# Source order on three more engines in the token mixers of a hybrid decoder layer, with projection weights loaded ahead, six streams and sums a tick later

## Chip, cores and metric

One core of one Trainium2 chip (trn2). The time is the device time of one execution in microseconds; lower is better. The kernel takes its inputs as they are and does all arithmetic on the chip in one launch.

## What is computed

One inference step of a decoder layer, width 1024, for a prompt of 1024 tokens and a sample group of 8 sequences with 4 new tokens each (32 columns), which share the weights. From the reference, cut:

```
h = x + 0.5 * _swiglu(_rmsnorm(x, g_ffn1), w_ffn1_in, w_ffn1_out)
u = _rmsnorm(h, g_mix)
z_swa, z_gq, z_gk, z_gv, z_gr, z_ga, z_mq = jnp.split(u @ w_in, SPLIT_POINTS, axis=-1)
# branch A, 3 groups (window, dilation) = (128,1), (512,4), (2048,16) x 4 heads of 128
q, k = _rope(qkv[:, :, 0], pos), _rope(qkv[:, :, 1], pos)
...  # per group: softmax over a band of 129 keys at stride dil, its output and log-denominator
o_swa = jnp.sum(softmax(stack(lses), axis=0)[..., None] * stack(outs), axis=0)
# branch B, gated linear attention: 4 heads, d_k 64, d_v 128, chunks of 64
# branch C, 4 heads of attention into 256 memory tokens
gates = jax.nn.sigmoid(u @ w_gate).reshape(B, T, N_BRANCH, D_MODEL)
h = h + jnp.sum(gates * einsum(stack([o_swa, o_gla, o_mem]), w_branch), axis=2) @ w_out
h = h + 0.5 * _swiglu(_rmsnorm(h, g_ffn2), w_ffn2_in, w_ffn2_out)
```

Prompt queries see the prompt's own keys. The sample's queries see cached keys and values of 8 sequences (up to 2048 positions in the third group, 256 memory positions in branch C), each sequence its own. All matrices are float32.

## The kernel before

The 1056 columns (1024 of the prompt, 32 of the sample) lie features on partitions, in NC = 3 chunks of C = 352. A float32 product is made of three matmuls on rounded halves: weights and activations are split into a high part and the rest, and `product` (L194 to L204) issues wh·xh (L202), wh·xl (L203) and wl·xh (L204) for each 128 rows of the contraction: 24 matmuls of 352 columns for a chunk of a projection out of `w_in`. `weights` (L177) makes the two halves: a load into `raw` (L174, issued by SyncE, SP), a cast on ScalarE into `whi` (L188), a subtraction on VectorE into `wlo` (L189). Each of the three tiles has two buffers (`WBUFS`). Big intermediate rows live in 34 slabs of 128 x 1056 floats, given out in turn, with a tag each use. PSUM has four `acc` and four `aux` buffers.

The mixers are the class `Mix`, its course in `run` (L1620): the four GLA heads with the memory projections, then for each head h and each group g a dilated-attention unit. `swa_unit` (L1301) makes the unit's three projections through `proj` (L778): weights first, then per chunk `tick`, `product`, and the evacuation. Queries and keys leave through `rope` (L1281): three VectorE products out of PSUM (L1289 to L1291), one sum on GpSimd (L1295), and a GpSimd sum for the sample's columns (L1297).

All else runs in **streams**: generators in five queues, of which `tick` (L100) advances each by one step before every chunk of a projection. So a unit of nine ticks carries, between its 24-matmul products, the steps of

- `swa_unit_attention` (L1321), the unit before: scores on TensorE (L1343) with a masked maximum on VectorE (L1348), softmax (VectorE nm L1353, ScalarE exponential L1356), transposes and their copies (pt, L1086 on ScalarE, L1088 on VectorE), values (L1384);
- `mem_head` (L1108), attention into the memory: scores, exponential (L1141), reciprocal and scaling (mml L1143, mp L1145), transposes, values (its inputs are split again: mqs, mpt L208, L209); behind it in the same queue `mem_sample` (L1185): products of cached memory keys and queries on GpSimd (mqb, L1204), their sums on VectorE (msc, L1205), transposes (L1211), a softmax (msp);
- `swa_sample_scores` (L1458): per cached sequence a load of the query rows and one of the cached keys into the slab kq (L1465, L1467, L1470), a product on GpSimd (kq, L1481), its sum on VectorE (ssc, L1482); `swa_sample` (L1488) then turns ssc on TensorE (L1494) and weighs the cached values (L1546);
- `swa_combine` (L1559): the three groups' weights (sd, cd and cb are trips through DRAM), products on VectorE and GpSimd (og, L1614) and sums on both (og, L1616).

TensorE takes the order in which the program is written (`manual_schedule` with PE alone, L1892). VectorE, ScalarE, GpSimd and SP take the order in which the framework's scheduler puts their instructions, by its own estimate of when each can run. `gated_branches` (L1650) follows; the last streams run on within it.

## Time and profile before

| | us |
|---|---|
| median of 3 runs | 3043.07 (3041.36 to 3049.46) |
| profiled execution | 3053.2 |
| its span on the core | 3051.4 |
| granted TensorE clock, mean over the span | 0.975 |
| busy: VectorE, ScalarE, GpSimd | 1415.2, 1013.6, 972.3 |

The span is read from the start of the execution's first instruction. A little after 790 us the GLA part begins, dilated attention runs from about 1100 to 1757, the gated branches from there to 1860; the feed-forward halves lie ahead and behind. Since one engine is busy nearly all the time, its waits and its clock are to be read, and of the others only what ends such a wait.

### The profile page before, as it was taken

The numbers are of one execution on the slowest core, as the hardware profiler recorded it, in microseconds if no ns is written. First come the engines' busy times: TensorE is split into PE (matmuls) and PEld (weight loads), VectorE is DVE, ScalarE is ACT, GpSimd is POOL, SyncE is SP. The second block draws the span as 40 slices with busy tenths as digits, with TensorE's granted clock in tenths as the row PEclk, the third lists the DMA queues.
The fourth block names the chain that finished last, engine by engine and source line by source line (L and its number), as shares of the span: only waits on it lengthen the run. The fifth ranks groups of instructions, "written<-read, shape, count | busy, mean of one in ns | idle before, by whom it ended". The sixth has DMA issues, their size and how long they took to land. (4 is left out here: it accounts for less than half of the span.)

```text
span 3051.4 us, 51965 instructions
## 1 busy us (share of the span) xinstructions
PE 2932.9 (96%) x21035; PEld 2867.0 (94%) x21035; DVE 1415.2 (46%) x2581; ACT 1013.6 (33%) x2007; POOL 972.3 (32%) x835
## 2 busy tenths in 40 slices
PE   8999999999999999899998889999999999999999
PEld 7999999899999999888897789999999999999998
DVE  7544444454424445656556551213246544444544
ACT  5433333221345433232332321212234433333212
POOL 4533331110401114637447350112236433332000
PEclk9999999999999999999999889999999999999999
DMA  5222224432211124666566563211252222225322
GB/s 180 80 73 82 78 79 154 151 119 67 92 43 57 58 71 131 174 164 195 150 182 189 166 189 105 81 42 56 75 168 85 78 78 82 73 78 194 96 62 86
DMA packets 455604, 332.88 MB, mean 109 GB/s; under 512 B 34850, under 2 KB 417284, under 8 KB 455364
## 3 DMA queue, kind: packets, MB, share of 16 engines
q1 hardware_dynamic: 445698, 323.44, 34.9%
q10 hardware_dynamic: 9666, 6.11, 0.7%
q8 instruction: 165, 2.70, 0.4%
q14 instruction: 75, 0.61, 0.1%
HBM read 268.88 MB, written 60.60 MB: 108 GB/s over the span
## 5 line engine op out<-in xcount | busy, mean ns | idle before, releaser
L202 PE MATMUL acc<-xh,whi 128*128 128x352 f32 x1776 | 600.0, 338 | 1.4 <-ACT whi L188 1.0
L204 PE MATMUL acc<-xh,wlo 128*128 128x352 f32 x1776 | 587.6, 331 | 8.1 <-DVE wlo L189 8.1
L203 PE MATMUL acc<-xl,whi 128*128 128x352 f32 x1776 | 586.0, 330 | 0.0
L202 PEld LDWEIGHTS acc<-xh,whi 128*128 128x128 f32 x1776 | 345.8, 195 | 13.5 <-issue 9.5
L204 PEld LDWEIGHTS acc<-xh,wlo 128*128 128x128 f32 x1776 | 344.4, 194 | 13.9 <-DVE wlo L189 13.9
L203 PEld LDWEIGHTS acc<-xl,whi 128*128 128x128 f32 x1776 | 345.4, 194 | 0.2
L188 ACT CAST whi<-raw 128x512 fp32r<-128x512 f32 (+2 forms) x200 | 163.3, 816 | 541.1 <-PE acc L203 467.6
L202 PE MATMUL acc<-hh,whi 128*128 128x352 f32 (+2 forms) x968 | 313.8, 324 | 3.0 <-ACT mv L628 1.6
L203 PE MATMUL acc<-hl,whi 128*128 128x352 f32 (+2 forms) x968 | 312.9, 323 | 2.9 <-POOL hl L209 2.1
L204 PE MATMUL acc<-hh,wlo 128*128 128x352 f32 (+2 forms) x968 | 312.9, 323 | 0.9 <-DVE wlo L189 0.9
L189 DVE TENSOR_TENSOR wlo<-raw,whi 128x512 fp32r<-128x512 f32 (+2 forms) x200 | 221.2, 1106 | 176.0 <-ACT whi L188 157.4
L202 PE MATMUL acc<-xs,swf 128*128 128x264 f32 x960 | 276.1, 288 | 8.6 <-ACT u L430 8.6
L203 PE MATMUL acc<-xs,swf 128*128 128x264 f32 x960 | 274.7, 286 | 0.0
L204 PE MATMUL acc<-xs,swf 128*128 128x264 f32 x960 | 274.6, 286 | 0.0
L662 DVE SCALAR_TENSOR_TENSOR h<-acc,h 128x352 f32<-128x352 f32 (+3 forms) x296 | 150.2, 512 | 220.8 <-PE acc L204 219.7
L202 PE MATMUL acc<-xs,whi 128*128 128x264 f32 x768 | 220.9, 288 | 2.5 <-ACT xs L208 1.9
L203 PE MATMUL acc<-xs,whi 128*128 128x264 f32 x768 | 220.8, 288 | 0.8 <-POOL xs L209 0.8
L202 PEld LDWEIGHTS acc<-xs,swf 128*128 128x128 f32 x960 | 182.3, 190 | 9.9 <-ACT u L430 9.9
L202 PEld LDWEIGHTS acc<-hh,whi 128*128 128x128 f32 x968 | 182.8, 189 | 4.3 <-ACT mv L628 1.9
L203 PEld LDWEIGHTS acc<-hl,whi 128*128 128x128 f32 x968 | 182.9, 189 | 3.6 <-POOL hl L209 2.3
L204 PEld LDWEIGHTS acc<-hh,wlo 128*128 128x128 f32 x968 | 182.8, 189 | 1.2 <-DVE wlo L189 1.2
L203 PEld LDWEIGHTS acc<-xs,swf 128*128 128x128 f32 x960 | 182.8, 190 | 0.0
(427 smaller groups left out, 6743.5 us busy)
## 6 DMA issues: line engine op xcount, KB each, us to landing
raw<-in_w_ffn_in SPq DMA_DIRECT2D x88, 512.0 KB, 3.9
raw<-in_w_in SPq DMA_DIRECT2D x52, 512.0 KB, 3.9
kq<-sqt SPq DMA_DIRECT2D x96, 256.0 KB, 5.5
hraw<-hidd SPq DMA_DIRECT2D x44, 528.0 KB, 3.9
raw<-in_w_ffn_out SPq DMA_DIRECT2D x64, 256.0 KB, 2.8
kq<-in_cache_swa SPq DMA_DIRECT2D x64, 256.0 KB, 5.1
vc<-in_cache_swa SPq DMA_DIRECT2D x64, 256.0 KB, 4.6
raw<-in_w_gate SPq DMA_DIRECT2D x24, 512.0 KB, 4.2
```

What stands on the lines that cost most here:

```text
L188: nc.scalar.copy(hi[:, :n], raw[:, :n])
L189: nc.vector.tensor_sub(lo[:, :n], raw[:, :n], hi[:, :n].bitcast(F32))
L202: mm(ps, wh[k], xh[k], start=first and k == 0, stop=False, skip_group_check=more)
L203: mm(ps, wh[k], xl[k], start=False, stop=False, skip_group_check=more)
L204: mm(ps, wl[k], xh[k], start=False, stop=last and k == n - 1, skip_group_check=more)
L662: nc.vector.scalar_tensor_tensor(hv, ps, scale, hv, op0=ALU.mult, op1=ALU.add)
```

## The change

It does four things.

1. `Mix.run()` stands in a second `manual_schedule` with VectorE, ScalarE and GpSimd: within the mixers these three issue in source order as well. SP does not, nor do the three engines in the gated branches or the feed-forward halves.
2. The projections after the first four are a list (`order`). `fetch` issues the raw load of the one after next in the first chunk of a projection, `prepare` casts and subtracts the next one's weights after the first chunk's evacuation; the last weights made in `gla_begin` go into slabs.
3. The streams have names and are six: `mem_sample` has a queue of its own ("cached") beside `mem_head`.
4. Steps are cut elsewhere: a sum (ssc, msc) stands one tick behind its GpSimd product, the last one at the end of the unit's last tick; the memory head scales its probabilities after a `yield`, the memory sample after one more; `swa_sample` begins two steps later and scales one later; a unit's softmax stands ahead of the next quad's scores (its scores one step before); in the combine the second product takes in the third on GpSimd, and VectorE adds the sum one step later.

```diff
-QUOTA = (1, 1, 1, 1, 1)
+STREAMS = ("attention", "memory", "windows", "cached", "scores", "combine")
...
-    def proj(self, *parts):
+        self.todo, self.raw, self.ready = deque(self.order()), deque(), deque()
+    def fetch(self):
+        if self.todo:
+            col, n = key = self.todo.popleft()
+            self.raw.append((key, self.k.raw_weights(self.wi[:, :, col:col + n], KD, n)))
+    def prepare(self, slabs=False):
+        if self.raw:
+            key, raw = self.raw.popleft()
+            self.ready.append((key, self.k.weights(None, KD, key[1], slabs=slabs, raw=raw)))
+    def proj(self, col, n, evac):
         k = self.k
-        ws = [k.weights(self.wi[:, :, col:col + n], KD, n, slabs=i > 0) for i, (col, n, _) in enumerate(parts)]
+        key, w = self.ready.popleft()
         for c in range(NC):
-            for w, (col, n, evac) in zip(ws, parts):
-                k.tick()
-                ps = k.acc()[:n, :C]
-                k.product(ps, w, chunk(self.u, c))
-                evac(ps, c)
+            k.tick()
+            if c == 0:
+                self.fetch()
+            ps = k.acc()[:n, :C]
+            k.product(ps, w, chunk(self.u, c))
+            evac(ps, c)
+            if c == 0:
+                self.prepare()
...
@@ gla_begin
+            if c == 1:
+                self.fetch()
+                self.fetch()
+                self.prepare(slabs=True)
...
@@ mem_sample (swa_sample_scores alike)
-            nc.vector.reduce_sum(sc[:, :, b * DT:(b + 1) * DT], s, axis=AX.X)
+            if b:
+                nc.vector.reduce_sum(sc[:, :, (b - 1) * DT:b * DT], last, axis=AX.X)
+            last = s
             yield
+        nc.vector.reduce_sum(sc[:, :, (DB - 1) * DT:], last, axis=AX.X)
...
@@ swa_unit_attention
         scores(0)
         yield
+        softmax(0)
         values_to_tokens(0)
         scores(1)
-        softmax(0)
-        yield
+        yield
+        softmax(1)
         e0 = transposes(0)
         values_to_tokens(1)
-        softmax(1)
         yield
...
@@ swa_combine
-            (nc.gpsimd if g else nc.vector).tensor_mul(o, o, w)
-            if g:
-                (nc.vector if g == 1 else nc.gpsimd).tensor_add(first, first, o)
+            (nc.gpsimd if g else nc.vector).tensor_mul(o[g], o[g], got.popleft())
+            if g == G - 1:
+                nc.gpsimd.tensor_add(o[1], o[1], o[2])
+                yield
+                nc.vector.tensor_add(o[0], o[0], o[1])
...
-                    k.streams[2].append(self.mem_head(h, mqd))
-                    k.streams[2].append(self.mem_sample(h))
+                    k.streams["memory"].append(self.mem_head(h, mqd))
+                    k.streams["cached"].append(self.mem_sample(h))
...
-    Mix(k, u[0], od, ktd, vd, g_gla).run()
+    with tc.manual_schedule(engines={mybir.EngineType.DVE, mybir.EngineType.Activation, mybir.EngineType.Pool}):
+        Mix(k, u[0], od, ktd, vd, g_gla).run()
```

How the order moves, at three places. In each row stand the line, the operation and what is written from what; line numbers of the changed kernel are one lower near its top and 29 to 48 higher in `Mix`. First **GpSimd**, where the memory sample's products (mqb) begin to run among those of the cached keys (kq) and the rope sums (q). Before, this is beside the first unit of the next head:

```order
L1481 TENSOR_TENSOR kq<-kq 128x512 x2
L1204 TENSOR_TENSOR mqb<-mqb,mkc 128x512 x2
L1481 TENSOR_TENSOR kq<-kq 128x512
L1204 TENSOR_TENSOR mqb<-mqb,mkc 128x512 x2
L1295 TENSOR_TENSOR q<-rp_14030,rp_14031 128x352
L1481 TENSOR_TENSOR kq<-kq 128x512
L1204 TENSOR_TENSOR mqb<-mqb,mkc 128x512
L1295 TENSOR_TENSOR q<-rp_14101,rp_14102 128x352
L1481 TENSOR_TENSOR kq<-kq 128x512
L1204 TENSOR_TENSOR mqb<-mqb,mkc 128x512 x2
L1295 TENSOR_TENSOR q<-rp_14163,rp_14164 128x320
```

and with the change beside the second unit of its own head:

```order
L1521 TENSOR_TENSOR kq<-kq 128x512 x2
L1335 TENSOR_TENSOR q<-rp_12806,rp_12807 128x4x88
L1240 TENSOR_TENSOR mqb<-mqb,mkc 128x512 x2
L1521 TENSOR_TENSOR kq<-kq 128x512
L1335 TENSOR_TENSOR q<-rp_12881,rp_12882 128x4x88
L1240 TENSOR_TENSOR mqb<-mqb,mkc 128x512 x2
L1521 TENSOR_TENSOR kq<-kq 128x512
L1335 TENSOR_TENSOR q<-rp_12965,rp_12966 128x4x80
L1337 TENSOR_TENSOR smp<-rp_12965,rp_12966 128x32
```

Before, seven products (kq, mqb) stand ahead of the first rope sum of q; now a rope sum stands behind every tick's products.

**ScalarE**, where a unit's v is projected: the casts of the next weights (whi) beside the copies of v's three chunks. Before:

```order
L1446 DMA out_swa_sample<-stok 64x1x128
L188 CAST whi<-raw 128x1024
L791 COPY v<-acc 128x352 x2
L188 CAST whi<-raw 128x1024
L791 COPY v<-acc 128x352
```

and with the change:

```order
L1486 DMA out_swa_sample<-stok 64x1x128
L820 COPY v<-acc 128x352
L187 CAST whi<-raw 128x1024
L820 COPY v<-acc 128x352 x2
L187 CAST whi<-raw 128x1024
```

In both, the copy-out of the sample's new rows stands ahead. Before, a cast stands ahead of all three copies and the next ahead of the third; now one stands behind the first copy and the next behind the third (in the next projection's first chunk, which leaves through VectorE).

**VectorE**, the last third of a head's combine (og, 320 columns) and a unit's score maxima (pq, stat). Before:

```order
L189 TENSOR_TENSOR wlo<-raw,whi 128x1024
L1482 TENSOR_REDUCE ssc<-kq 128x4
L1614 TENSOR_TENSOR og<-og,cb 128x320
L1482 TENSOR_REDUCE ssc<-kq 128x4
L1616 TENSOR_TENSOR og<-og 128x320
L1348 ISA pq,stat<-aux,band 128x128
L1348 ISA stat 128x1
L1348 ISA pq,stat<-aux,band 128x256
L1348 ISA stat 128x1
```

and with the change:

```order
L1659 TENSOR_TENSOR og<-og,cb 128x320
L1329 TENSOR_TENSOR rp_15668<-acc,cos 128x352
L1330 TENSOR_TENSOR rp_15669<-acc,sin 64x352
L1331 TENSOR_TENSOR rp_15669<-acc,sin 64x352
L1523 TENSOR_REDUCE ssc<-kq 128x4
L1527 TENSOR_REDUCE ssc<-kq 128x4
L1663 TENSOR_TENSOR og<-og 128x320
L188 TENSOR_TENSOR wlo<-raw,whi 128x1024
L1388 ISA pq,stat<-aux,band_10557 128x128
```

Before, the combine's product and the sum that takes in a GpSimd product are one row apart, with the maxima right behind; now a whole tick, with three rope products and two sums of cached keys, stands between them, and the weights' subtraction (wlo) behind, ahead of the maxima.

## Rows read from the trace of the kernel before

**Rows 1.** The page's first part: busy time of each engine, its share of the span and its instructions.

```profile
PE 2932.9 (96%) x21035; PEld 2867.0 (94%) x21035; DVE 1415.2 (46%) x2581; ACT 1013.6 (33%) x2007; POOL 972.3 (32%) x835
```

**Rows 2.** Busy time by stretch, from the start of the span: head 0 of dilated attention (1100 to 1325 us), heads 1 to 3 (to 1757), the gated branches (to 1860). Columns: the stretch, its length, busy time and instructions of each engine, the mean granted clock of TensorE, the share of the DMA engines and GB/s.

```profile
1100.00:1325.00 225.00, 209.14 (x1351) 203.31 (x1350) 129.99 (x273) 79.89 (x178) 102.65 (x81) 0.96 0.49 134
1325.00:1757.00 432.00, 390.25 (x2977) 367.76 (x2977) 249.44 (x556) 133.49 (x327) 218.59 (x175) 0.94 0.63 179
1757.00:1860.00 103.00, 91.46 (x709) 85.28 (x708) 42.80 (x66) 26.01 (x42) 42.87 (x35) 0.92 0.61 184
```

**Rows 3.** TensorE's waits in head 0 (1100 to 1325 us): tile and line that waited, what it waited for, us in total, times, the longest.

```profile
PE aux L1231 <- DVE msp L1218: 4.8, 1, 4.8
PE aux L1134 <- ACT mqs L208: 4.0, 2, 2.3
PE aux L1179 <- DVE mp L1145: 3.7, 1, 3.7
```

**Rows 4.** The same in heads 1 to 3 (1325 to 1757 us).

```profile
PE aux L1211 <- DVE msc L1205: 12.8, 2, 8.3
PE aux L1343 <- DVE stat L1348: 9.9, 3, 4.0
PE aux L1413 <- ACT mp L1141: 4.7, 1, 4.7
PE aux L1384 <- DVE pt L1088: 4.0, 1, 4.0
```

**Rows 5.** The same in the gated branches (1757 to 1860 us).

```profile
PE aux L1494 <- DVE ssc L1482: 4.4, 1, 4.4
PE acc L204 <- DVE wlo L189: 4.4, 2, 3.8
```

**Rows 6.** The timeline of VectorE and TensorE from 1440 to 1457 us, in head 1: start, duration, engine, line, operation, what is written from what, and in brackets the idle time before it with what ended it.

```profile
1440.75 1.53 DVE L1616 TENSOR_TENSOR og<-og 128x320 f32<-128x320 f32 x1 [4.24 <-POOL og L1614]
...
1442.89 1.13 PE L1343 MATMUL aux<-k,q 128*128 128x256 f32 x4 [2.09 <-DVE stat L1348]
1452.31 0.61 PE L1211 MATMUL aux<-ident,msc 128*32 128x128 f32 x2 [8.29 <-DVE msc L1205]
...
1455.95 0.49 PE L204 MATMUL acc<-xh,wlo 128*128 128x352 f32 x1
1456.24 0.41 PE L202 MATMUL acc<-xh,whi 128*128 128x352 f32 x1
...
1456.81 0.32 PE L202 MATMUL acc<-xh,whi 128*128 128x352 f32 x1
1456.97 0.32 PE L203 MATMUL acc<-xl,whi 128*128 128x352 f32 x1
```

**Rows 7.** The stretches in which TensorE's granted clock stands at 0.50 or 0.51, by the same view as rows 2: its line of sums over the four such stretches of head 0, the six of heads 1 to 3, the three of the gated branches. First the length of all, then the busy time in them, then means.

```profile
sum 17.00, PE 16.32 PEld 15.13 DVE 10.99 ACT 1.00 POOL 7.15; mean PE 4.08 PEld 3.78 DVE 2.75 ACT 0.25 POOL 1.79
...
sum 47.70, PE 28.68 PEld 25.19 DVE 32.69 ACT 14.16 POOL 28.08; mean PE 4.78 PEld 4.20 DVE 5.45 ACT 2.36 POOL 4.68
...
sum 17.00, PE 15.20 PEld 14.33 DVE 10.29 ACT 0.79 POOL 13.60; mean PE 5.07 PEld 4.78 DVE 3.43 ACT 0.26 POOL 4.53
```

**Rows 8.** Waits of the DMA queue's engine (SPq), of ScalarE and of GpSimd from 1100 to 1860 us, columns as in rows 3.

```profile
SPq L174 <- DVE wlo L189: 162.0, 28, 13.1
...
ACT whi L188 <- PE acc L203: 85.7, 24, 10.5
...
POOL kq L1481 <- DMA kq<-in_cache_swa: 123.1, 43, 10.4
```

**Rows 9.** Groups of instructions of one line and one shape from 1100 to 1860 us, on GpSimd, VectorE and ScalarE: count, then busy time in us and mean ns of one, then the idle time before them and what ended it.

```profile
L1481 POOL TENSOR_TENSOR kq<-kq 128x512 f32<-128x512 f32 x96 | 126.6, 1323 | 142.3 <-DMA kq<-in_cache_swa 123.1 <-ACT v L791 7.0 <-DMA kq<-sqt 6.4
L1204 POOL TENSOR_TENSOR mqb<-mqb,mkc 128x512 f32<-128x512 f32 x64 | 86.8, 1373 | 4.6 <-DMA mkc<-in_cache_mem_kv 4.2
L1295 POOL TENSOR_TENSOR q<-rp,rp 128x352 f32<-128x352 f32 x22 | 29.9, 1359 | 114.5 <-DVE rp L1291 112.1 <-ACT vt L1366 2.3
...
L1295 POOL TENSOR_TENSOR q<-rp,rp 128x320 f32<-128x320 f32 x11 | 23.0, 2094 | 37.4 <-DVE rp L1291 37.4
...
L1482 DVE TENSOR_REDUCE ssc<-kq 128x4 f32<-128x512 f32 x96 | 65.4, 682 | 111.6 <-POOL kq L1481 111.2
L189 DVE TENSOR_TENSOR wlo<-raw,whi 128x1024 fp32r<-128x1024 f32 x39 | 55.7, 1428 | 17.8 <-ACT whi L188 17.2
L1205 DVE TENSOR_REDUCE msc<-mqb 128x8 f32<-128x1024 f32 x32 | 38.7, 1211 | 20.4 <-POOL mqb L1204 20.4
...
L1289 DVE TENSOR_TENSOR rp<-acc,cos 128x352 f32<-128x352 f32 x66 | 34.2, 519 | 45.2 <-PE acc L204 44.5 <-DMA mqb<-mqt 0.5
...
L1145 DVE TENSOR_SCALAR mp<-mp,mml 128x256 f32<-128x256 f32 x32 | 14.7, 502 | 0.5
...
L1069 ACT ACT_TABLE_LOAD x5 | 6.4, 1283 | 1.4 <-PE acc L204 1.2
```

**Rows 10.** The instructions on the tile kq (cached keys and the sample's query) from 1100 to 1860 us: durations in ns, least, median, largest; and the time from issue to landing of its loads.

```profile
L1465 SPq DMA_DIRECT2D kq<-sqt x96: 319/456/2132, 1139.7 to 1798.5; - x96
...
DMA to landing us min/median/max: 3.2/5.1/8.4
```

**Rows 11.** Two lines' instructions in the same stretch, durations in ns, least, median, largest.

```profile
L1145 DVE TENSOR_SCALAR mp<-mp,mml x32: 341/352/2319, 1135.8 to 1769.6; 128x256 f32<-128x256 f32 x32
...
L1295 POOL TENSOR_TENSOR k<-rp,rp x33: 868/1472/3047, 1140.9 to 1708.3; 128x352 f32<-128x352 f32 x22, 128x320 f32<-128x320 f32 x11
```

More of the change, by code (lines that the diff above doesn't have):

```diff
@@ L96, in __init__ @@
         nc.gpsimd.memset(self.half, -0.5)
-        self.streams = [deque() for _ in QUOTA]
+        self.streams = {n: deque() for n in STREAMS}
         self.later = deque()
     def tick(self):
-        for q, s in zip(QUOTA, self.streams):
-            for _ in range(q):
-                while s:
-                    try:
-                        next(s[0])
-                        break
-                    except StopIteration:
-                        s.popleft()
+        for s in self.streams.values():
+            while s:
+                try:
+                    next(s[0])
+                    break
+                except StopIteration:
+                    s.popleft()
     def step(self):
@@ L124, in flush @@
     def flush(self):
-        while any(self.streams):
+        while any(self.streams.values()):
             self.tick()
@@ L776, in __init__, with order @@
         self.wi = k.A["w_in"][0].rearrange("(k p) f -> p k f", p=128)
[L778 removed]
+        self.todo, self.raw, self.ready = deque(self.order()), deque(), deque()
+    def order(self):
+        v = [(COL_GV + i * E, E) for i in range(H)]
+        m = [(COL_MQ + i * E, E) for i in range(H)]
+        r = [(COL_GR + i * E, E) for i in range(H)]
+        out = [v[1], m[0], (COL_GQ + 128, 128), (COL_GK + 128, 128), v[2], v[3], m[1], m[2], m[3], r[0], r[1]]
+        for h in range(H):
+            for g in range(G):
+                out += [(c + (g * H + h) * E, E) for c in (COL_Q, COL_K, COL_V)]
+                if h == 0 and g < 2:
+                    out.append(r[2 + g])
+        return out
+    def fetch(self):
[7 more added lines that the diff above has]
+    def proj(self, col, n, evac):
         k = self.k
[L782 removed]
+        key, w = self.ready.popleft()
+        assert key == (col, n)
         for c in range(NC):
[L784 to L788 removed]
+            k.tick()
[6 more added lines that the diff above has]
+                self.prepare()
     def copy_to(self, s):
@@ L1160, in mem_head @@
             if i < 4:
-                p = scores(i * 256)
+                p, l = scores(i * 256)
                 if i < 3:
@@ L1448, in swa_unit_attention @@
         head[g] = dict(st=st, og=og, smp=smp, vtok=vtok)
-        k.streams[1].append(self.swa_sample_scores(h, g, head))
+        k.streams["scores"].append(self.swa_sample_scores(h, g, head))
         if g == G - 1:
-            k.streams[4].append(self.swa_combine(h, head))
+            k.streams["combine"].append(self.swa_combine(h, head))
     def cache_rows(self, g, kv, h, b):
@@ L1481, in swa_sample_scores @@
             nc.gpsimd.tensor_mul(q, q, kv)
-            nc.vector.reduce_sum(head["sc"][:, g, b * DT:(b + 1) * DT], q, axis=AX.X)
+            if b:
+                nc.vector.reduce_sum(head["sc"][:, g, (b - 1) * DT:b * DT], last, axis=AX.X)
+            last = q
             if b < DB - 1:
                 yield
+        nc.vector.reduce_sum(head["sc"][:, g, (DB - 1) * DT:], last, axis=AX.X)
         if g == G - 1:
-            k.streams[3].append(self.swa_sample(h, head))
+            k.streams["windows"].append(self.swa_sample(h, head))
     def swa_sample(self, h, head):
@@ L1606, in swa_combine @@
         for n, (i, g) in enumerate(todo):
-            if n % 3 == 0:
+            o = [head[x]["og"][:, part(i)] for x in range(G)]
+            if g == 0:
                 yield
@@ L1626, in run @@
         on = []
-        k.streams[0].append(self.gla(0, *self.gla_proj(0, qk), on))
+        k.streams["attention"].append(self.gla(0, *self.gla_proj(0, qk), on))
         self.mem_proj(0, mqd)
@@ L1631, in run @@
         k.flush()
-        k.streams[0].append(self.gla(1, *z, on))
+        k.streams["attention"].append(self.gla(1, *z, on))
         self.mem_proj(2, mqd)
@@ L1641, in run @@
                 z = self.swa_unit(h, g)
-                k.streams[0].append(self.swa_unit_attention(h, g, head, *z))
+                k.streams["attention"].append(self.swa_unit_attention(h, g, head, *z))
                 if h == 0 and g < 2:
@@ L1793, in build @@
     store_h(1, h)
-    Mix(k, u[0], od, ktd, vd, g_gla).run()
+    with tc.manual_schedule(engines={mybir.EngineType.DVE, mybir.EngineType.Activation, mybir.EngineType.Pool}):
+        Mix(k, u[0], od, ktd, vd, g_gla).run()
     m = gated_branches(k, u[0], od, (1, 2, 0))
-    assert not any(k.streams)
+    assert not any(k.streams.values())
     if stop == 2:
```

21 lines of the change are left out of this document (12 added, 9 removed).

## The prediction

> **What bounds the kernel now.** TensorE: the page's first part has it busy for 96% of the span [rows 1]. What a change of order can win is therefore what TensorE waits and what it computes at half clock, so I read first the busy time by stretch, then TensorE's waits in each, then its clock, and only then the queues behind the waits.
>
> By stretch, in the part that the changed order reaches beside the GLA heads [rows 2]: head 0 of dilated attention (225 us) leaves TensorE 15.9 us idle, heads 1 to 3 (432 us) 41.8, the gated branches (103 us, the last streams still run there) 11.5. In sum 69.2 us in 760.
>
> What ends these idle times is nearly always VectorE [rows 3 to 5]: in heads 1 to 3 the memory sample's scores, the scores' row maxima, copies of probabilities. That is not because VectorE is full (249 of 432 us) but because it stands in a queue behind GpSimd. One place shows it [rows 6]: the scheduler has put the combine's product and sum ahead of the row maxima; VectorE waits 4.24 us for GpSimd there, TensorE waits 2.09 us for the maxima, and then 8.29 us for the msc sum, which came last of four late jobs.
>
> The second loss is the clock. After the 8.29 us TensorE's 352-column steps are 0.29 us apart, where they were 0.16 a few steps later [rows 6]: 1.2 GHz in place of 2.4. The stretches of granted clock 0.50 hold 16.3 us of TensorE work in head 0, 28.7 in heads 1 to 3, 15.2 in the gated part [rows 7]. At full clock each would need 0.16/0.29 of it, so 45.7% is lost: 7.5, 13.1 and 6.9 us. Idle and clock together: 23.4, 54.9 and 18.4, that is **96.7 us**, the most that a new order can give here.
>
> **The change part by part.** The profiled execution took 3053.2 us, 10.1 more than the median 3043.07 of the runs; the sum is made against 3053.2 and the forecast then put 10.1 lower.
>
> *Weights ahead.* Nothing is added: the same loads, casts and subtractions. SP waits 162 us for a raw buffer (a wlo not yet subtracted) with the cached keys' loads behind it, and ScalarE's cast waits 86 us for the last matmul on its whi, with copies and exponentials behind it [rows 8]. With the raw load two ahead and the cast after the first chunk, both buffers are free when asked for: these two waits go. TensorE itself hardly waited for weights (wlo 4.4 us, in the gated part, which is not touched [rows 5]), so the direct gain is 0; the indirect one is in the sums below. The new price: VectorE's subtraction (1.43 us [rows 9]) stands between a chunk's rope and the next tick's jobs; it is in the tick sums below.
>
> *Stated order, later sums and six streams* go together, as one sum of work per tick (a tick is a turn of all streams and then one chunk of 24 matmuls, 24 x 0.16 = 3.8 us, plus the streams' own matmuls, taken at an estimated 0.11 us from their columns against 352). In source order no instruction of VectorE, ScalarE or GpSimd stands behind a later tick's, so a TensorE wait comes only where the work of a few ticks exceeds TensorE's.
>
> - GpSimd. Before, its order put up to seven products ahead of a rope sum; now a tick holds three or four of its instructions. The heaviest six ticks of a head are those of q and k in its second unit, where the memory head, the memory sample, the combine of the head before and the first unit's cached keys all run: 6 x 1.32 (kq) + 10 x 1.37 (mqb) + 4 x 1.36 + 2 x 1.97 (rope) + 0.9 (sample columns) = 31.9 us [rows 9] (the sample columns, and the 320-column sums of k, are smaller groups of that view).
> - TensorE in the same six: 6 x 3.82 + 66 small x 0.112 = 30.3 us, 5.05 a tick.
> - VectorE: 18 rope products x 0.52 = 9.4; 6 kq sums x 0.68 = 4.1; 4 msc sums x 1.21 = 4.8; 2 wlo 2.8; the memory head's steps 7.5; 8 score maxima 3.2; the combine's chain 2.8; the rest 2.5: **37.0 us** [rows 9] (its smaller groups likewise). Separated from its GpSimd product by a tick, a sum no longer waits; but VectorE is 6.7 us behind TensorE by itself. Before, the scheduler spread this over a head.
> - The first four ticks of the third unit, where `swa_sample` and the combine's og products come in: VectorE 28.0 against TensorE's 23.2, by the same means.
>
> *Head 0* has one heavy tick (VectorE 6.9, GpSimd 7.9, TensorE 5.8) and a nearly empty one behind it. The waits [rows 3] for the memory head's copies and for msp get a tick more by the moved yields. What I leave: 3 us (a load of cached memory values), 1.5 of GpSimd's surplus, 2.5 of clock, so 7 of 23.4: **gain 16.4**.
>
> *Heads 1 to 3.* Per head: 6.7 behind, less some 2 us by which a consumer stands later than its producer: 4.8. Second hump 4.8 less 2: 2.8. And the fetch: of 96 kq fetches some 23 take, in the new order, a slab of the 34 whose last reader on TensorE stands in the tick of the fetch's own use (before: 3). From that matmul on it takes two issues of 0.46, a landing of 5.1 and the product's 1.32 [rows 9, 10] = 7.3 us, against a tick of 5.05. GpSimd is then late by 2.3, VectorE's sum is a tick later anyway, but the last sum of a unit follows its product in the same tick: 4 us a head. Together 11.6 x 3 = 35. For the clock I leave 13, as now: idle of several us stays in each head, and after such idle the clock fell [rows 6, 7]. 48 of 54.9: **gain 7**.
>
> *Gated part.* The ssc wait (4.4) goes: two more yields stand before its reader; wlo (4.4) stays; clock follows in part: 9 of 18.4: **gain 9.5**.
>
> *GLA heads.* Source order alternates the functions of ScalarE where the scheduler had grouped them: four more table loads of 1.28 us [rows 9] on an engine that waits more than it works: **loss 2**, bounds 0 and 5.
>
> Sum 16.4 + 7 + 9.5 - 2 = 31; 3053.2 - 31 = 3022, on the median's scale **3012 us**. Bounds of the unknown terms: heads 1 to 3 gain 35 if a head's lag is absorbed by later ticks, lose 20 if each late fetch reaches TensorE.
>
> **A rule against it.** A single scaling of the memory probabilities takes 0.35 us in the median and 2.3 at most, a rope sum on GpSimd 0.87 at least, 1.5 in the median and 3.0 at most [rows 11]: something that is not their own size holds them up. If VectorE's instructions with both operands in SBUF (in the six ticks wlo 2.7, mqs 1.7, the combine 2.8, the scaling 2.0 = 9.2 us) could not run beside GpSimd's products, the six ticks would need 31.9 + 9.2 = 41.1 us, 10.8 behind TensorE instead of 6.7. The Trainium skill, "SBUF — State Buffer", section "Who interferes with whom", says that VectorE and GpSimd share a pair of ports under an exclusive lock, that a VectorE instruction with two SBUF inputs contends with a GpSimd one that reads SBUF, and that the other blocks fully. By that rule the packed order pays twice; no row here separates a lock from other causes.
>
> **The rivals.**
> 1. *The lag is absorbed.* VectorE's 37.0 and 28.0 are means taken while GpSimd worked beside it; what is behind is caught up in the lighter ticks between the two humps, and TensorE's readers stand late enough. For it: VectorE has 58% of the time in heads 1 to 3 [rows 2]. Against: 6.7 us is over one tick. Only some 20 of the 96.7 us stay: 3053 - 75 - 10 = 2968.
> 2. *Blocking counts.* 3.8 us more a head x 3, and some 4 of clock: gain 15, 3028.
> 3. *The waits change places.* Each head's surplus of both humps reaches TensorE whole and takes the clock along, some 20 us a head: 96.7 stays what it was: 3043. For it: the amount of work on each engine is the same.
> 4. *Slower: late fetches.* Place: kq fetches of heads 1 to 3 and GpSimd's fixed order. In stated order GpSimd waits at its kq product with the rope sums behind it, and TensorE's scores need those; GpSimd already waits 123 us for these loads in 43 places [rows 8], now with no later work put ahead. 21 late fetches x 2.0 us = 42 cancel the gain (12 of them are in the sum); at 2.7 to 4 us each, with the clock, 15 to 42 us slower: about 3075. For it: 2.3 us is the median case, landings reach 8.4 [rows 10]. Against: SP is free of its 162 us of waits, so fetches go out earlier.
>
> That the order isn't what is said is no rival: after the change only 5 places of these three engines in the mixers depart from source order, against 348 before.
>
> **How the numbers follow.** Forecast 0.42 (own range 2985 to 3033), rival 1 0.15, rival 2 0.08, rival 3 0.14, rival 4 0.21. Low 2965 takes in rival 1, high 3065 half of rival 4. A measurement tells 0.3%, 9 us, from no change: faster is 0.42 + 0.15 + 0.08 = 0.65, same 0.14, slower 0.21.
>
> **What would show it.** Right: SP's waits at the raw load and ScalarE's at the cast vanish; no TensorE wait for msc, and ssc only at a unit's end; what remains lies in a head's second unit and the first half of its third and ends with VectorE's pq, pt or mpt; head 0 runs nearly without idle. Rival 1: TensorE idle in heads 1 to 3 under 10 us, granted clock 0.98 there. Rival 2: VectorE's and GpSimd's mean durations rise where they overlap. Rival 4: GpSimd's kq waits for its loads are over 150 us and precede TensorE's waits for q or k. The forecast is wrong as a whole if heads 1 to 3 are longer than 445 or shorter than 400 us.

## The result

| | median us | runs | ratio to before, 95% interval |
|---|---|---|---|
| before | 3044.98 | 4 | |
| changed | 3084.11 (3079.91 to 3090.28) | 4 | 1.0125 (1.0111 to 1.0139) |

The change makes the kernel 1.25% slower, where 1% faster was forecast. The profiled execution took 3079.91 us, its span is 3078.1. It is the fastest of its four runs, and that of the kernel before (3053.2) took 8 us more than its median: the two profiles are 27 us apart, the medians 39, so lengths read against the profile of before can flatter the other kernel by several us. TensorE's busy time is what it was (2936.3 us, 2932.9 in [rows 1]); it is its idle time that grew.

Where: the stretches of [rows 2] are cut at TensorE's start of certain matmuls of the projections. The same matmuls, counted by number, give these stretches of the changed kernel (from matmul to matmul the stretches of the kernel before are 310.0 us, the GLA heads, then 224.0, 432.9 and 103.0):

```profile
786.10:1103.00 316.90, 304.90 (x1971) 288.82 (x1970) 122.43 (x226) 141.20 (x219) 42.91 (x47) 0.94 0.19 57
1103.00:1324.90 221.90, 204.97 (x1349) 198.57 (x1347) 127.12 (x259) 80.83 (x177) 98.99 (x76) 0.98 0.47 128
1324.90:1790.40 465.50, 404.23 (x3043) 377.28 (x3043) 276.50 (x591) 134.74 (x339) 238.49 (x192) 0.93 0.63 176
1790.40:1881.90 91.50, 81.77 (x584) 77.29 (x583) 30.24 (x51) 17.23 (x27) 24.91 (x22) 0.94 0.58 170
```

So the GLA heads are 6.9 us longer, head 0 2 shorter, heads 1 to 3 33 longer, the gated branches 11 shorter. The last two belong together: the six streams end sooner, and some 10 us of TensorE's work moved from the gated part (91.5 to 81.8 us busy) into the heads (390 to 404). Idle time in heads 1 to 3 went from 42 to 61 us.

TensorE's waits in heads 1 to 3, which answer to [rows 4]:

```profile
PE aux L1215 <- DVE mp L1181: 18.9, 7, 5.2
PE aux L1250 <- ACT pt L1119: 12.6, 3, 4.4
PE aux L1383 <- DVE stat L1388: 6.0, 1, 6.0
PE aux L1115 <- DVE stat L1388: 4.2, 3, 2.1
```

The wait for msc is gone and so is that for ssc; but L1250, the very transposes that waited for msc (L1211 before), now wait as long for something else, ScalarE's copy pt, and L1215, the transposes of the memory head's probabilities, wait for their scaling mp. The long ones (4.1 to 4.4 us for pt, 4.5 to 5.2 for mp) come at the same two places in each of heads 1 to 3. The queues behind them, from head 0 to the gated part, answer to [rows 8]:

```profile
SPq L173 <- DVE wlo L188: 162.4, 32, 14.2
...
ACT whi L187 <- PE acc L202: 27.9, 10, 6.4
...
POOL kq L1521 <- DMA kq<-in_cache_swa: 104.4, 33, 9.7
...
DVE mqs L208 <- ACT mqs L207: 37.9, 13, 6.6
```

SP's wait at the raw load has not changed at all (162.4, 162.0 before); ScalarE's at the cast has fallen to a third; VectorE has a new one, for ScalarE's mqs.

**Place one**, in a head's third unit (head 2 here), timeline of GpSimd, VectorE, ScalarE and TensorE:

```profile
1533.12 2.45 POOL L1335 TENSOR_TENSOR q<-rp,rp 128x352 f32<-128x352 f32 x1 [4.90 <-DVE rp L1331]
...
1534.21 1.39 DVE L1393 TENSOR_SCALAR nm<-stat 128x4 f32<-128x4 f32 x1
...
1535.68 0.40 ACT L1396 ACTIVATE pq<-pq,nm 128x128 f32<-128x128 f32 x1 [4.55 <-POOL q L1335]
...
1536.42 1.29 PE L1115 MATMUL aux<-ident,pq 128*128 128x128 f32 x4 [2.07 <-DVE stat L1388]
...
1541.68 0.17 DVE L1393 TENSOR_SCALAR nm<-stat 128x4 f32<-128x4 f32 x1
...
1541.89 0.51 ACT L1396 ACTIVATE pq<-pq,nm 128x256 f32<-128x256 f32 x1 [3.60 <-DVE nm L1393]
...
1543.87 0.56 ACT L1119 COPY pt<-aux 128x512 f32<-128x512 f32 x1
...
1544.49 0.61 PE L1250 MATMUL aux<-ident,msc 128*32 128x128 f32 x2 [4.13 <-ACT pt L1119]
...
1545.19 0.49 PE L202 MATMUL acc<-xl,whi 128*128 128x352 f32 x1
...
1545.48 0.49 PE L203 MATMUL acc<-xh,wlo 128*128 128x352 f32 x1
```

The negated maxima of the scores, nm, stand on VectorE behind a tick of its work; the first took 1.39 us beside a rope sum on GpSimd that took 2.45. ScalarE's exponentials wait for nm (the view names the rope sum, which ended at the same time), TensorE 2.07 us for them. Then ScalarE stands at the second softmax, again for nm (3.60 us), and only behind its four exponentials comes the copy pt of the first quad (1543.87). That copy holds one of the streams' four PSUM buffers, so the memory sample's transposes wait 4.13 us, though their own input is long there (msc's last sum ended at 1530.5). Behind it the steps are 0.29 us apart: half clock (granted clock 0.55 in the mean from 1544.75 to 1549.00).

**Place two**, in its second unit, the same engines and SP:

```profile
1492.06 0.84 SPq L1637 DMA_DIRECT2D cd<-ce  x1
...
1496.52 0.81 SPq L1647 DMA_DIRECT2D cb<-cd  x2
...
1499.51 0.38 SPq L1229 DMA_DIRECT2D mqb<-mqt  x1
...
1499.66 0.33 ACTq L1485 DMA_DIRECT2D sqt<-stok  x1
...
1501.09 0.58 ACTq L1486 DMA_DIRECT2D out_swa_sample<-stok  x1
...
1501.80 0.47 ACT L1174 ACTIVATE mp<-aux,mmx 128x256 f32<-128x256 f32 x1 [7.32 <-DMA mkc<-in_cache_mem_kv]
...
1503.14 0.42 DVE L208 TENSOR_TENSOR mqs<-mqo,mqs 128x256 fp32r<-128x256 f32 x1 [5.80 <-ACT mqs L207]
...
1506.38 2.60 POOL L1240 TENSOR_TENSOR mqb<-mqb,mkc 128x512 f32<-128x512 f32 x2 [6.33 <-DMA mqb<-mqt]
...
1507.03 2.11 DVE L1181 TENSOR_SCALAR mp<-mp,mml 128x256 f32<-128x256 f32 x2
...
1507.94 0.45 PE L1215 MATMUL aux<-ident,mp 128*128 128x128 f32 x1 [5.00 <-DVE mp L1181]
```

SP issues cd's store at 1492.06, then stands until 1496.5 for it to come back (cb reads it from DRAM); mqb's load goes out at 1499.51 and GpSimd waits 6.33 us for it. ScalarE stands 7.3 us ahead of its exponentials, in two small stores of the new sample rows. In the trace all 1178 DMAs share eight completion semaphores (147 or 148 on each), and an issue waits for the DMA that had its semaphore before, whatever queue that one is on: the first store went out at 1499.66, when the load of cb that SP had issued at 1496.52 had landed (1499.59), the second at 1501.09, when a load of mkc, also SP's, had landed (1501.07). So the first store, too, stood behind SP's trip through DRAM. VectorE stands behind ScalarE (5.80 us for mqs), TensorE behind VectorE (5.00).

### The profile page after: what moved, and what is told of

Same layout as the page of the kernel before. It is cut to its first block, busy times and chain, and to the rows that moved or that the text cites. A ratio compares the mean times of both kernels' runs of the same rounds, so it can differ in the third digit from the quotient of the medians.

```text
span 3078.1 us, 51999 instructions
## 1 busy us (share of the span) xinstructions
PE 2936.3 (95%) x21035; PEld 2864.8 (93%) x21035; DVE 1430.4 (46%) x2581; ACT 1011.1 (33%) x2007; POOL 970.4 (32%) x835
## 4 chain that ended last, share of the span: by engine, by line
PE 47%; DVE 4%; POOL 3%; DMA 3%; issue 2%; ACT 2%; SPq 0%; POOLq 0%; DVEq 0%; ACTq 0%
PE acc L201 14%; PE acc L203 14%; PE acc L202 14%; DMA kq<-in_cache_swa 1%; POOL mqb L1240 1%; ACT pq L1396 1%; POOL kq L1521 1%; PE aux L201 1%; PE aux L202 1%; PE aux L203 1%; DVE wlo L188 1%; PE aux L1424 1%; PE aux L1592 0%; POOL q L1335 0%; DMA cb<-cd 0%
## 5 line engine op out<-in xcount | busy, mean ns | idle before, releaser
L201 PE MATMUL acc<-xh,whi 128*128 128x352 f32 x1752 | 592.0, 338 | 1.0 <-ACT whi L187 1.0
L203 PE MATMUL acc<-xh,wlo 128*128 128x352 f32 x1752 | 580.0, 331 | 8.8 <-DVE wlo L188 8.8
L202 PE MATMUL acc<-xl,whi 128*128 128x352 f32 x1752 | 578.5, 330 | 0.0
L188 DVE TENSOR_TENSOR wlo<-raw,whi 128x1024 fp32r<-128x1024 f32 (+2 forms) x199 | 217.8, 1094 | 187.7 <-ACT whi L187 168.8
L187 ACT CAST whi<-raw 128x1024 fp32r<-128x1024 f32 (+2 forms) x199 | 162.3, 816 | 400.4 <-PE acc L202 375.3
L201 PE MATMUL acc<-xs,whi 128*128 128x264 f32 x768 | 220.9, 288 | 2.5 <-ACT xs L207 1.9
L202 PE MATMUL acc<-xs,whi 128*128 128x264 f32 x768 | 220.7, 287 | 0.8 <-POOL xs L208 0.8
L201 PEld LDWEIGHTS acc<-xs,swf 128*128 128x128 f32 x960 | 181.8, 189 | 10.1 <-ACT u L429 10.1
L203 PE MATMUL acc<-xs,whi 128*128 128x264 f32 x640 | 182.0, 284 | 0.5 <-DVE whi L208 0.5
```

The costliest lines, as they stand in the source:

```text
L187: nc.scalar.copy(hi[:, :n], raw[:, :n])
L188: nc.vector.tensor_sub(lo[:, :n], raw[:, :n], hi[:, :n].bitcast(F32))
L201: mm(ps, wh[k], xh[k], start=first and k == 0, stop=False, skip_group_check=more)
L202: mm(ps, wh[k], xl[k], start=False, stop=False, skip_group_check=more)
L203: mm(ps, wl[k], xh[k], start=False, stop=last and k == n - 1, skip_group_check=more)
```

## Experiments

Ratios are to the kernel before, run beside each on the same chip. "Heads" is the length from head 0 to the end of the gated part in the one profiled execution, cut at the same matmuls: 759.9 us before, 778.8 in the changed kernel. "GLA" is the GLA heads, 310.0 before. Since the profile of before is a long execution, the ratios decide, and the lengths tell where.

**Which engines' order it is.** One line of the change is edited, e.g. for e5:

```diff
-    with tc.manual_schedule(engines={mybir.EngineType.DVE, mybir.EngineType.Activation, mybir.EngineType.Pool}):
+    with tc.manual_schedule(engines={mybir.EngineType.DVE, mybir.EngineType.Pool}):
```

e1 drops the line; e8 keeps ScalarE alone, e10 VectorE and ScalarE, e11 ScalarE and GpSimd. All other parts of the change stay.

e1: 

> The changed kernel, but VectorE, ScalarE and GpSimd are ordered by the scheduler again; the list of projections, six streams and moved sums stay. Theory A (ScalarE's fixed order makes the loss: it stands behind DMA issues of its own, and its copies of probabilities stand behind later exponentials): the scheduler puts them elsewhere, 3035 to 3055 us. Theory B (VectorE's sum of work per tick, the term of the prediction): the scheduler spreads it again, also 3035 to 3055. Theory C (the memory sample in a stream of its own packs more into a head's second unit, whatever the order): stays above 3070.

e5: 

> The changed kernel with only VectorE and GpSimd in source order in the mixers; ScalarE is ordered by the scheduler. Theory A: both losses of a head go, 3040 to 3055 us. Theory B: within 8 us of 3084. Theory C: above 3070.

e8: 

> The changed kernel with ScalarE alone in source order in the mixers; VectorE and GpSimd are ordered by the scheduler. Theory A: ScalarE's order is what costs: 3070 to 3090. Theory B or D (the fixed order of VectorE and GpSimd is needed for the loss): below 3060.

e10: 

> The changed kernel with VectorE and ScalarE in source order in the mixers, GpSimd ordered by the scheduler. Theory A2 (the loss is made by ScalarE and VectorE together: the copies of probabilities stand on ScalarE behind exponentials that need a maximum nm, which stands on VectorE behind a tick's whole work): 1.009 to 1.013 of before. Rival (GpSimd's fixed order, through late loads, is part of it): below 1.005.

e11: 

> The changed kernel with ScalarE and GpSimd in source order in the mixers, VectorE ordered by the scheduler. Theory A2: no pair that waits on each other is left, 0.998 to 1.004 of before. Rival: over 1.008.

| in source order | ratio | interval | heads us | GLA us |
|---|---|---|---|---|
| none (e1) | 1.0025 | 1.0009 to 1.0040 | 758.0 | 308.5 |
| ScalarE (e8) | 1.0007 | 0.9997 to 1.0017 | 751.7 | 307.5 |
| VectorE, GpSimd (e5) | 0.9999 | 0.9982 to 1.0016 | 727.3 | 321.6 |
| ScalarE, GpSimd (e11) | 1.0023 | 1.0009 to 1.0036 | 743.5 | 325.4 |
| VectorE, ScalarE (e10) | 1.0158 | 1.0140 to 1.0176 | 794.3 | 316.0 |
| all three (changed) | 1.0125 | 1.0111 to 1.0139 | 778.8 | 316.9 |

Neither ScalarE's order costs by itself (e8) nor VectorE's with GpSimd's (e5): only ScalarE and VectorE together do, by 1.2 to 1.6%. VectorE's order alone was not run; that it takes both engines is shown with GpSimd in order (e5 and e11 against all three). Theory A as it was first put (ScalarE's order by itself) is wrong by e8, B by e5, C by e1; A2, the two engines waiting for each other, stands, though e10 lost more than its 0.9 to 1.3%: GpSimd in source order takes off some of the loss. Streams, weights ahead and later sums with the scheduler's order gain nothing (e1, 0.25% slower).

**Place one.** e3 puts a unit's softmax back, e7 takes the PSUM buffer away as a cause and leaves the order:

```diff
e3, swa_unit_attention
         yield
-        softmax(0)
         values_to_tokens(0)
         scores(1)
+        softmax(0)
         yield
-        softmax(1)
         e0 = transposes(0)
         values_to_tokens(1)
+        softmax(1)
e7, mem_sample
-        ps = k.aux()[:NS, :MEM]
+        ps = k.acc()[:NS, :MEM]
```

e3: 

> The changed kernel with only a unit's softmax back at its old places: the first behind the next quad's scores, the second behind the transposes of the first. Theory A: in ScalarE's order the copies of probabilities (pt) stand ahead of the second softmax's exponentials again, so the memory sample's transposes no longer wait 4.1 us for a PSUM buffer in each of heads 1 to 3, and the clock stays up behind it: 20 to 30 us faster, 3055 to 3065. Theory B: VectorE has the same work per tick, within 8 us of 3084. Theory C: as theory B.

e7: 

> The changed kernel, but the memory sample's turned scores take a PSUM buffer of the projections (acc) in place of one of the streams' four (aux), so that they need not wait for ScalarE's copy of the probabilities. Theory A: the wait of 4.1 to 4.4 us in each of heads 1 to 3 goes and with it 4 to 5 us of half clock: 3058 to 3072 us. Rival: the next reader of ScalarE's late copies takes the wait a tick later: within 8 us of 3084.

e3 1.0068 (1.0046 to 1.0090; heads 763.7), e7 1.0069 (1.0048 to 1.0090; 767.2). TensorE's longest waits in e7, same stretch:

```profile
PE aux L1215 <- DVE mp L1181: 23.9, 11, 5.3
...
PE aux L1115 <- DVE stat L1388: 5.7, 3, 2.1
```

L1250 no longer stands among them, and nothing of its size took its place. So the held buffer is shown, at 0.56% of the time, since e7 changes nothing else. Its source is the place of the softmax in source order: e3, which moves both softmaxes of a unit, gains the same 0.57%, and the timeline of place one names the second. The wait for mp is untouched by either (23.8 us in e3, 23.9 in e7; 22.5 in the changed kernel over the same stretch).

**Place two.** e4 has SP issue the two small stores (`nc.sync.dma_start` for `nc.scalar.dma_start` at L1485, L1486); e6 is e3 and e4 together; e9 begins the memory sample nine ticks later; e12 adds SP to the engines in source order; e13 is e12 and e3.

e4: 

> The changed kernel, but the two small stores of a unit's new sample rows (sqt and the sample's keys and values) are issued by SP, not by ScalarE. Theory A: ScalarE no longer stands 5 us at these issues in the second unit of heads 1 to 3, the memory head's exponentials come at once, and TensorE's wait of 4.5 to 5.2 us for the scaled probabilities goes, with part of the half-clock stretch behind it: 15 to 25 us faster, 3060 to 3070. Theory B: the scaled probabilities are late by VectorE's own work, within 8 us of 3084. Against both: SP's own queue takes the waits and the cached keys' loads come later, up to 10 us slower.

e6: 

> The changed kernel with both: a unit's softmax at its old places, and the stores of the new sample rows issued by SP. Theory A in its first form (two separate losses of ScalarE's order): a further 15 to 20 us below the 3061 of the softmax alone, 3041 to 3047. Theory D (the second loss is a chain from late loads: SP stands behind the combine's trips through DRAM, GpSimd's product waits for the load, VectorE's sum stands in order behind the product and the memory head's tiles behind the sum; ScalarE's issues were only one of two paths that end at the same time): within 6 us of 3061.

e9: 

> The changed kernel, but the memory sample begins nine ticks later, in a head's third unit. The sums in those ticks change: in the second unit GpSimd has 18 us in six ticks in place of 32, VectorE 32 in place of 37. Theory B or C (the packing of the second unit): the waits of the second unit go, 3055 to 3070, or less if the third unit takes them over. Theory A: the wait for the scaled probabilities (5 us a head) stays where ScalarE's issue stands, the wait of the sample's own transposes moves a unit further: within 10 us of 3084.

```diff
e9, mem_sample
+        for _ in range(9):
+            yield
         nxt = load(0)
e12
-    with tc.manual_schedule(engines={mybir.EngineType.DVE, mybir.EngineType.Activation, mybir.EngineType.Pool}):
+    with tc.manual_schedule(engines={mybir.EngineType.DVE, mybir.EngineType.Activation, mybir.EngineType.Pool, mybir.EngineType.SP}):
```

e12: 

> The changed kernel with SP in source order in the mixers as well. Theory D (the wait of some 5 us a head for the scaled probabilities comes from SP, which the scheduler lets stand at the combine's trips through DRAM and at raw loads, the other loads behind): SP's waits at the raw load and at al and cb go, GpSimd's waits for mqb and kq fall, the wait for the scaled probabilities goes; the wait for the PSUM buffer (4 us a head) stays: 1.004 to 1.009 of before. Rival (source order puts a kq or mqb load only a tick ahead of its use, and now nothing comes earlier): GpSimd's waits rise and it is over 1.0125.

e13: 

> As the one before, with a unit's softmax at its old places too: by theories A2 and D both losses of a head go, 0.990 to 0.998 of before; by the rival over 1.007, where the softmax alone stood.

e4 gave 1.0136 (1.0114 to 1.0158): nothing, where theory A wanted 15 to 25 us. Its waits and the place that took over (timeline, head 2):

```profile
PE aux L1383 <- DVE mpt L208: 13.8, 3, 5.9
PE aux L1250 <- ACT pt L1119: 13.1, 3, 4.4
...
PE aux L1215 <- DVE mp L1181: 7.3, 6, 1.7
```

```profile
1508.78 2.67 POOL L1240 TENSOR_TENSOR mqb<-mqb,mkc 128x512 f32<-128x512 f32 x2 [5.83 <-DMA mqb<-mqt]
...
1519.73 0.69 DVE L1527 TENSOR_REDUCE ssc<-kq 128x4 f32<-128x512 f32 x1 [4.71 <-POOL kq L1521]
...
1521.93 0.68 DVE L208 TENSOR_TENSOR mpt<-aux,mpt 128x512 fp32r<-128x512 f32 x1
...
1522.66 1.22 PE L1383 MATMUL aux<-k,q 128*128 128x128 f32 x4 [5.50 <-DVE mpt L208]
```

The wait for mp has fallen from 22.5 us to 7.3, but 13.8 stand at L1383 for mpt, where 1.4 stood: GpSimd waits 5.83 us for the load of mqb, the last sum of a unit (L1527) 4.71 for GpSimd's product in the same tick, the tile mpt stands behind it on VectorE. The loads were late in any case; ScalarE's stores were one of two ways to the same end. That is theory D, and e6 agrees (1.0083, 1.0058 to 1.0107; no lower than e3).

e9 closes the other way, GpSimd's late product of mqb in the second unit, by moving it to the third, and leaves ScalarE's stores where they are. It gave 1.0074 (1.0053 to 1.0096), but not where theories B and C said it: heads 1 to 3 stayed at 468 us and head 0 became 10 us shorter. The transposes of msc no longer wait for a buffer, but the wait for mp stays in the second unit, as theory A said, and is longer (5.4 to 7.0 us in each of heads 1 to 3), and waits for cached values (vc) grow from 3.5 to 12.2 us. So closing either way alone does not take the second loss away.

e12 gave 1.0074 (1.0049 to 1.0098; heads 762.9), e13 1.0033 (1.0017 to 1.0049; 750.1). TensorE and SP in e12:

```profile
PE aux L1250 <- ACT pt L1119: 12.4, 3, 4.4
...
PE aux L1215 <- DVE mp L1181: 7.9, 7, 1.7
PE aux L1115 <- ACT pq L1396: 7.2, 2, 3.7
```

```profile
SPq L173 <- DVE wlo L188: 63.8, 13, 13.5
...
SPq L1619 <- DMA sd<-stat: 10.4, 2, 8.1
```

In source order SP comes to al and cb three ticks after the stores, not at once: 10.4 us for sd in place of 41.7, and the waits for mp fall to 7.9, none over 1.7, with place one still at 12.4. GpSimd's waits at mqb fall from 29.4 us to 6.9. So D is shown in its main part; a cleaner pair, e16 and e18, follows. GpSimd's kq waits did not fall (129 us, 104 in the changed kernel), and SP's wait at the raw load fell but did not go: D had both too far. e13 missed the 0.990 to 0.998 of A2 and D together; its heads are 9.8 us shorter than before, but its GLA part is 326.0 us.

**The queries.** e14 exchanges two calls so that ScalarE's cast mqs is written ahead of the memory head's exponentials; e15 is e14 and e3.

```diff
-                p, l = scores(i * 256)
                 if i < 3:
                     queries(i * 256 + 256)
+                p, l = scores(i * 256)
```

e14: 

> The changed kernel with one pair of calls exchanged in the memory head: the next queries are split (ScalarE's cast mqs, VectorE's remainder) ahead of a step's scores, not behind its exponentials. Theory A3 (the other half of the loss: VectorE stands in order 37.9 us in 13 waits for ScalarE's mqs, which stands in ScalarE's order behind exponentials that wait for VectorE's own maximum): this wait falls under 10 us, heads 1 to 3 become 10 to 25 us shorter, 1.004 to 1.009 of before. Rival (the loads are late anyway and end at the same time, as with the rows by SP): over 1.010.

e15: 

> The same with a unit's softmax at its old places too, all three engines in source order. Theories A2 and A3: both places at which the two engines wait on each other within a tick are gone, heads 0 to 3 and the gated part as short as with ScalarE free (727 to 740 us; 779 in the changed kernel): 0.997 to 1.003 of before. Rival: the two do not add, 1.005 or more.

e14 1.0120 (1.0099 to 1.0141), e15 1.0083 (1.0068 to 1.0098). VectorE in e14:

```profile
DVE mqs L208 <- ACT mqs L207: 31.4, 8, 7.1
```

31.4 us in place of 37.9, and no gain: the place of the cast is not what VectorE waits for. A3 falls; that ScalarE is late there for other reasons is argued, not shown.

**Order in the heads alone.** The `with` stands around the loop over the heads in `run`, not around all mixers: e16 for VectorE and GpSimd, e17 for all three with e15's mends, e18 for VectorE, GpSimd and SP, e19 for all four with e3's.

```diff
-    with tc.manual_schedule(...):
-        Mix(k, u[0], od, ktd, vd, g_gla).run()
+    Mix(k, u[0], od, ktd, vd, g_gla).run()
... run
+        with k.tc.manual_schedule(engines={mybir.EngineType.DVE, mybir.EngineType.Pool, mybir.EngineType.SP}):
             for h in range(H):
```

e16: 

> The changed kernel with VectorE and GpSimd in source order in the attention heads alone; ScalarE everywhere and all three in the GLA part by the scheduler. If the loss of 7 to 15 us in the GLA part is due to source order there: GLA part 305 to 311 us, the rest as with ScalarE free, 0.993 to 0.998 of before. Rival (that loss is due to the changed streams and weights): 0.999 to 1.002.

e17: 

> All three engines in source order in the attention heads alone, softmax at its old places and queries split first. By theories A2 and A3 and with the GLA part by the scheduler: 0.993 to 0.999 of before; if the two mends do not add: over 1.000.

e18: 

> VectorE, GpSimd and SP in source order in the attention heads alone; ScalarE, and all four in the GLA part, by the scheduler. Theory D: the wait for the scaled probabilities (5 to 8 us a head, still there with ScalarE free) goes with SP's order; heads 0 to 3 and the gated part 700 to 725 us in place of 743 with SP by the scheduler: 0.985 to 0.994 of before. Rival (SP in source order waits elsewhere): 0.996 or more.

e19: 

> All four engines in source order in the attention heads alone, with a unit's softmax at its old places. By theories A2 and D, and the GLA part by the scheduler: 0.994 to 0.999 of before, the heads and the gated part about 750 us as with SP in order in all mixers. If the GLA part's loss were not from source order there: 1.002 or more.

| | ratio | interval | heads us | GLA us |
|---|---|---|---|---|
| e16 | 0.9979 | 0.9967 to 0.9992 | 743.4 | 314.6 |
| e17 | 1.0044 | 1.0028 to 1.0060 | 767.3 | 311.5 |
| e18 | **0.9909** | 0.9886 to 0.9932 | 716.3 | 317.7 |
| e19 | 1.0011 | 0.9998 to 1.0024 | 750.6 | 311.6 |

e18, 3019.75 us, is faster than both kernels. TensorE's waits in it:

```profile
PE aux L1115 <- ACT pq L1396: 8.7, 2, 5.2
PE acc L203 <- DVE wlo L188: 8.0, 2, 4.2
PE aux L1215 <- DVE mp L1181: 6.1, 6, 1.7
PE aux L1383 <- DVE stat L1388: 5.9, 1, 5.9
```

No wait for msc or ssc and no long one for a PSUM buffer, 6.1 us for mp in six short ones. Heads 1 to 3 have 27 us idle (42 before).

e16 and e18 differ by SP's order alone: 0.70% of the time, some 21 us. The late loads and the wait for mp go with it, first in e16:

```profile
POOL mqb L1240 <- DMA mqb<-mqt: 29.3, 4, 13.4
PE aux L1215 <- DVE mp L1181: 17.5, 5, 8.2
```

In e18 GpSimd waits 5.8 us at mqb, and SP 11.3 us for sd where it waited 51.2 in e16:

```profile
POOL mqb L1240 <- DMA mkc<-in_cache_mem_kv: 5.8, 3, 4.0
```

The distance of e18 to e19, which differs by ScalarE's order and the softmax's place, is 1.0%: about what ScalarE's order still costs with both mends. In the heads ScalarE waits 65.2 us for nm in e19 and 28.7 in e18:

```profile
ACT pq L1396 <- DVE nm L1393: 65.2, 21, 7.2
```

```profile
ACT pq L1396 <- DVE nm L1393: 28.7, 20, 2.7
```

That speaks for the same cause, exponentials that stand in order at a maximum of VectorE's with copies and casts behind them, at places other than place one. No run took these apart: it is argued, not shown (the changed kernel and e5, 38 us apart, differ in this wait by 11 us only, 42.4 and 31.0).

e17, 1.0044, missed its 0.993 to 0.999; by its own terms the two mends do not add. e19, 1.0011, lies between its two cases. In the GLA part source order costs: the pairs e5 and e16, e15 and e17, e13 and e19 differ by it alone, and it is 7.0, 14.6 and 14.4 us longer with the order. But e16 to e19 still stand at 311.5 to 317.7 us, where 305 to 311 were expected and 310.0 stood before; single executions differ by several us, and what the rest is stays open.

## Why the prediction was wrong

**What bounds the kernel** was read rightly: waits for VectorE's queue and the clock behind them are where an order gains; e18 gains there. Heads 1 to 3 took 465.5 us, past the 445 at which the prediction called itself wrong as a whole, and head 0, which was to run nearly without idle, kept 16.9 us of it (15.9 before).

**The step that failed** is "stated order, later sums and six streams go together, as one sum of work per tick ... a TensorE wait comes only where the work of a few ticks exceeds TensorE's". It left ScalarE out, as an engine that waits more than it works, and gave its order only 2 us of table loads. A sum of work says when an engine is full, not when two engines wait for each other within a tick. With ScalarE in order too, 1.26% is lost against e5, 38 us: 0.57% of it is the softmax's place (e3, and e7 by its buffer), the rest, 0.7%, stays open in its places; between e18 and e19 it is 1.0%. I had costed this at nothing.

The sum was too high without ScalarE as well. In e5's one profiled execution it seems to hold: head 0 12.1 us shorter (16.4 said), heads 1 to 3 6.1 (7), the gated part 14.4 (9.5), 32.6 together in place of 32.9. That agreement is in part luck: two of the three terms miss by 4 and 5 us in opposite ways, the execution of before is a long one, and over all runs e5 is no faster than before (0.9999), where the sum gave 1.0%. e16, with the same order in the heads, gained 16.5 us there and 0.21% in time. What it lacked most is SP's order: with SP in order too (e18) the kernel gains 0.9%, nearly what was forecast. An estimate from these ratios, taken in different runs: of the some 70 us between forecast and result 38 are ScalarE's order with VectorE's (e5 to the changed kernel), 21 SP's order (e16 to e18) and 6 source order in the GLA part (e5 to e16).

**Weights ahead.** ScalarE's wait at the cast fell, as said. SP's did not (162.4 us): SP stays with the scheduler, and only in source order does it fall (63.8 us in e12). "These two waits go" was wrong for SP, and with it the argument against the late loads.

**Late fetches.** The rival that ended slower had nearly the size (3075), but by luck: it left out ScalarE, without whose order nothing is lost (e5). It had one of the mechanisms, GpSimd in fixed order behind late loads, but put it at kq's slabs, and kq's waits fell (104 us, 123 before [rows 8]), where its sign was over 150. What is late is mqb's load, and beside it ScalarE's stores, and what makes both late is SP at the combine's trips through DRAM.

**msc, ssc.** Those waits went, as said; the transposes of msc wait as long for a buffer.

**GLA heads.** 2 us said, bounds 0 and 5; 6.9 in the changed kernel and up to 16 in others with source order there. Four table loads more are there, as said (39, 35 before), and they explain only 5 us at most. TensorE has a new wait there; no run took it apart:

```profile
PE aux L1065 <- ACT gtok L1057: 6.5, 2, 3.9
```

**Blocking.** The scaling mp takes 0.84 us in the mean, where it took 0.50 [rows 9], and the 352-column rope sums of q 1.84 where they took 1.36:

```profile
L1181 DVE TENSOR_SCALAR mp<-mp,mml 128x256 f32<-128x256 f32 x32 | 25.7, 842 | 0.6
...
L1335 POOL TENSOR_TENSOR q<-rp,rp 128x352 f32<-128x352 f32 x22 | 40.5, 1842 | 146.7 <-DVE rp L1331 146.7
```

So both are longer where they are packed side by side, by 11 us over the 32 scalings. But in e18, the fastest kernel, they take 0.95 and 1.83 us: this is not what makes the loss.

Two slips in the prediction's working are small: 0.16/0.29 leaves 44.8% lost, not 45.7 (0.5 us in the sum), and rival 2's 41.1 us is 4.1 above the 37.0, not 3.8.

## What to carry to other kernels

Before an order is fixed on several engines, follow each place at which two of them wait for each other within one step (a maximum on one, the exponential on the other, the copy behind it), and ask what stands behind each wait: a fixed order costs where a wait has ready work behind it. Cost every engine that is put in order, the one with spare time too; here the one that serves many streams, ScalarE, did best with the scheduler (e18). Try the DMA issuer in the same order as the engines that wait for its loads: here, left to the scheduler, it stood at a DRAM round trip with other loads behind, and its order was worth 0.7%. And where two causes end at the same time, taking one away shows nothing (e4): take both.

## What was not expected of the hardware

A small store on ScalarE's queue stood 5.2 us before its issue in place two (6.3 in head 0), for a load that SP had issued. Taken from the end of ScalarE's instruction before each, the 24 issues of these stores stood 23.5 us in the changed kernel and 7.5 in e12, with SP in source order. They also stood 29.8 us in the kernel before and 35.1 in e5, which is no slower than it: how long the stores stand does not by itself tell what they cost.

The scaling of four maxima (nm) took 1.39 us on VectorE beside a rope sum on GpSimd that took 2.45; elsewhere it took 0.17 (1541.68 in place one). All 24 of the changed kernel show what decides. In ten cases a GpSimd product or sum was running when nm began; these took 0.91 to 1.51 us, and each ended 0.02 to 0.03 us after the GpSimd instruction. In nine the GpSimd instruction began 0.04 to 0.05 us after nm, and nm took 0.17, as it did in the five others (0.16 to 0.17; in one of them the GpSimd instruction began 0.01 us before). The Trainium skill, "SBUF — State Buffer", section "Who interferes with whom", says that `tensor_scalar` on VectorE can enter modes that use both pairs of ports, and that whichever of it and a GpSimd instruction issues first then has the shared pair for the whole instruction while the other is blocked; the ten and the nine cases agree.
